# A hybrid decoder layer on one core: the second norm's 1/rms moved from the operand of the expert scores to the scores themselves

## The chip, the core and the metric

The program runs on one core of a Trainium2 chip. The metric is device time in microseconds, from start to end of one execution. Three runs of the kernel before took 4057.06, 4062.6 and 4065.22 us; the median is 4062.6.

The engines named here: TensorE (PE in the rows; PEld its weight loads), VectorE (DVE), ScalarE (ACT), GpSimd (POOL), SyncE (SP). Each works through its own instructions in order. DMAs are issued from the queues of SP, ScalarE (ACTq) and GpSimd.

## The reference

One layer of a decoder for 512 tokens of width 2048, all float32, and a final norm:

```python
h = rms_norm(x, norm_mix)
hq, hf, hi, hog, mq, mkv, mkr, ga, gb = split(h @ w_in)
o_a = hgrn2_branch(hq, hf, hi, hog, ...)            # (512, 1024)
o_b = mla_branch(mq, mkv, mkr, ...)                 # (512, 1024)
y = sigmoid(ga) * (o_a @ w_a) + sigmoid(gb) * (o_b @ w_b)
x = x + y @ w_o
x = x + peer_ffn(rms_norm(x, norm_ffn), peer_wq, k1, k2, u_tab, v_tab)
hp = rms_norm(x, norm_ple)
x = x + sigmoid(hp @ w_pg) * (p @ w_pe)
return rms_norm(x, norm_final)
```

`peer_ffn` on the normalised h: queries q = h @ peer_wq, for 8 heads two halves of 128; scores of the halves against 128 keys each; the best 16 of each half, of their 256 sums the best 16; a softmax over these gives the gates. An expert is a row of two tables of 16384 x 2048: the result is the sum over the chosen experts e of gate_e * gelu(u_e . h) * v_e.

## The kernel before

**Precision and weights.** A float32 matrix product is made of three products of rounded parts (`mm3`, L151 to L153): each operand is split into a rounded high part and the rest, the low part. A block of weights is 128 x 2048; it comes in two halves of 512 KB (L107, on SP's queue, `raw`), ScalarE rounds each half (L115, `hi`) and VectorE subtracts (L116, `lo`). There are four tiles of each kind, so two blocks. A block of 16 chunks with 256 columns is 48 products on TensorE.

**Two halves of the tokens.** After the mixers, the tokens go in two halves of 256, A and B. Half A goes through `merge_half` (gates, `w_a`, `w_b`), `residual_half` (`w_o`, x1 = x + y @ w_o), `embed_half` (`w_pe`), and `scores_half` (`wq`, keys). Of half A the first 160 tokens are served by gathering expert rows (128 in `eA`, 32 more in `eX`), the others (NE = 96) and half B (together ND = 352) by dense products over all experts. The order of this part is chosen by the framework's scheduler. Half B then follows under a written order (`manual_schedule`): gates of half B from `xB` (`w_ga`, `w_gb`, 16 blocks each), merge, residual, embeddings, scores. `ahead.step()` loads two blocks ahead and splits one ahead; `run_late()` issues what the block before left over (evacuations, splits); `background()` issues a share of a list `todo`: the top-16 work of 128 tokens (`prep_A`, then `prep_B`), and dot products of gathered rows with h (`dot_u`, L929). `phase` spreads the costs of the list over a number of blocks: here one list over 80 blocks, with `NEARLY` = 26 row dot products mixed into `prep_B`.

**The norm around which the change lies.** `residual_half` writes x1 to its own tile (L690), adds up squares (L235, L236) and stores x1 (L692). `embed_half` multiplies the embeddings of its half and, amid them, sums the squares over the features on TensorE (L206), makes 1/rms (`rstd_cols`) and spreads it over rows (`rows_of`, L215 to L220). Only then `h_chunk` (L723) makes t = x1 * gain * (1/rms) chunk by chunk, and `split` (L158, L159) its high and low part for the scores. `rows_of_h` (L829 to L834) later adds high and low parts of half A again and transposes them to rows (`hrow`, `hrowX`) for the gathered experts.

**Mixers' outputs.** In the second 16 gate blocks of half B, `mixed` (L646) issues on ScalarE's queue the load of a mixer output of 128 x 256 and splits it at once (L158, L159, into `ohB`, `olB`).

**After that.** 128 blocks of `uT` (dense z for ND tokens), with the rest of the row dot products and the gate matrices; then 16 groups of 8 blocks `vB`, with all 160 row updates (L1222), and the last norms and gate. Short-lived tiles of up to 128 x 512 come from `t2()`, a ring of six.

Of the kernel before, what the change touches and what calls it, by code (L numbers as in the profile page):

```python
# [10 lines left out]
F32 = mybir.dt.float32  # L11
# [9 lines left out]
T = 512  # L21
# [29 lines left out]
def kernel(ctx: ExitStack, tc: tile.TileContext, a, dbg=None):  # L51
# [218 lines left out]
    pe_s = [[dram.tile([128, 2, H], F32, name=f"pe{h}_{i}") for i in range(8)] for h in range(2)]  # L270
# [408 lines left out]
    def residual_half(hf, yh, yl, x1, sq):  # L679
        s = slice(hf * H, hf * H + H)  # L680
        for mt in range(16):
# [15 lines left out]
    def p_half(hf, ph, pl):  # L697
        for k in range(2):
            r = t2()[:, :H]
            nc.sync.dma_start(r, a["pT"][k][:, hf * H:hf * H + H])  # L700
            split(ph[:, k], pl[:, k], r)

    def embed_half(hf, ph, pl, sq, rr):

        for i in range(2):
            w = block(a["w_pe"][i])
            for m in range(0, 8, 2):
                ps = mx()
                for c in range(2):
                    for k in range(2):  # L710
                        mm3(ps[:, c * H:c * H + H], *w.part((m + c) * 2 + k, 16), ph[:, k], pl[:, k], k == 0, k == 1)
                t = t2()
                S.activation(t, ps, AF.Copy)
                nc.scalar.dma_start(flat(pe_s[hf][i * 4 + m // 2]), t)
                if (i, m) == (0, 2):
                    rc = rstd_cols(sums_over_features(sq.acc), D, "rc_ffn")
                if (i, m) == (1, 2):
                    rows_of(rc, rr)
            done()

    def h_chunk(k, x1, rr, hh, hl, kept=None):
        t = t2()[:, :H]
        V.scalar_tensor_tensor(t, x1[:, k], g_ffn[:, k:k + 1], rr, op0=OP.mult, op1=OP.mult)  # L723
        split(hh, hl, t)
        if kept is not None:
            nc.scalar.dma_start(kept, t[:, NA + NX:])

    def scores_half(hf, hh, hl):
# [3 lines left out]
        def keys(i, q):  # L732
# [782 lines left out]
```

## Time and profile before

| | |
|---|---|
| median of 3 runs | 4062.6 us |
| the profiled execution | 4065.97 us, its span 4064.2 us, mean granted clock 0.986 |
| TensorE busy | 3948.1 us (97% of the span), 24921 products |
| VectorE busy | 2946.7 us (73%) |
| ScalarE busy | 1744.0 us (43%) |
| GpSimd busy | 528.8 us (13%) |
| DMA | 1013.75 MB, 249 GB/s over the span |

TensorE's busy time counts products that overlap, so a busy stretch need not be one at full rate; the granted clock (PEclk, 1.00 for 2.4 GHz, 0.50 for 1.2) is a mean over a stretch. The boundaries of the windows below are those of the stages: first half's residual (985.6 to 1076.1), its embeddings and scores (to 1202.9), gates of the second half (to 1441.9; the second 16 blocks from about 1318), merge (to 1548.2), residual (to 1641.0), embeddings and scores (to 1788.1; the scores alone at their steady rate from 1701.9), and the groups of `vB` (2841.1 to 3862.0).

### The profile page before, as it was taken

Reading aid. Unit: us, or ns where it says so; the run is one execution under the profiler, and the core shown is the slowest. Engines: PE = TensorE matmul, PEld = TensorE weight load, DVE = VectorE, ACT = ScalarE, POOL = GpSimd, SP = SyncE. Lnnn points to the kernel's source line nnn. Section 1 sums busy time; section 2 is a strip of 40 time slices with the busy share of each in tenths; the row PEclk is TensorE's granted clock in tenths of the full one; section 3 lists DMA queues with packets and bytes.
Section 4 is the critical chain, followed back from the end, with each engine's and each line's share of the span. In section 5 each row is a group of like instructions: output and inputs, shape, how many; then the busy total and the mean of one; then the engine's idle time right before and its main releaser. Section 6 shows DMA issues by size and latency. Waiting matters only on the chain. (4 is left out here: it accounts for less than half of the span.)

```text
span 4064.2 us, 63784 instructions
## 1 busy us (share of the span) xinstructions
PE 3948.1 (97%) x24921; PEld 3742.2 (92%) x24921; DVE 2946.7 (73%) x4421; ACT 1744.0 (43%) x2800; POOL 528.8 (13%) x326
## 2 busy tenths in 40 slices
PE   9999999999989789899999999999999999999998
PEld 7878788899989789799999999999999999999986
DVE  5352565556638588768989898886898898889844
ACT  5242443445434334445455456663333333333443
POOL 0000000000000011012222222221222232222000
PEclk9999999999999999899999999999999999999999
DMA  5222234367766678688888888889999999999632
GB/s 211 93 78 94 68 113 130 127 202 238 225 191 192 213 264 277 228 288 291 304 320 305 307 300 315 325 309 350 355 360 354 345 358 359 363 344 357 212 117 96
DMA packets 317772, 1013.75 MB, mean 249 GB/s; under 512 B 32544, under 2 KB 134432, under 8 KB 274592
## 3 DMA queue, kind: packets, MB, share of 16 engines
q1 hardware_dynamic: 226624, 596.33, 43.4%
q0 software_dynamic: 46080, 335.56, 21.5%
q10 hardware_dynamic: 44768, 77.79, 5.1%
q8 instruction: 197, 3.23, 0.3%
q14 instruction: 103, 0.84, 0.1%
HBM read 933.27 MB, written 76.28 MB: 248 GB/s over the span
## 5 line engine op out<-in xcount | busy, mean ns | idle before, releaser
L116 DVE TENSOR_TENSOR lo<-raw,hi 128x1024 fp32r<-128x1024 f32 x970 | 1168.6, 1221 | 671.0 <-ACT hi L115 666.1
L115 ACT ACTIVATE hi<-raw 128x1024 fp32r<-128x1024 f32 x970 | 1015.7, 1056 | 1227.4 <-PE acc L152 891.0
L151 PE MATMUL acc<-hBh,hi 128*128 128x352 f32 (+1 forms) x2304 | 746.8, 324 | 3.1 <-ACT hBh L158 2.5
L153 PE MATMUL acc<-hBh,lo 128*128 128x352 f32 (+1 forms) x2304 | 742.1, 322 | 0.5 <-DVE lo L116 0.5
L152 PE MATMUL acc<-hBl,hi 128*128 128x352 f32 (+1 forms) x2304 | 739.2, 321 | 0.2
L922 POOL DMA_INDIRECT row<-in_peer_u_dram,eA x128 | 211.8, 1655 | 2351.8 <-DVE eA L942 1394.2
L151 PEld LDWEIGHTS acc<-hBh,hi 128*128 128x128 f32 x2304 | 436.7, 190 | 7.4 <-ACT hBh L158 7.4
L152 PEld LDWEIGHTS acc<-hBl,hi 128*128 128x128 f32 x2304 | 435.9, 189 | 3.0 <-DVE hBl L159 3.0
L153 PEld LDWEIGHTS acc<-hBh,lo 128*128 128x128 f32 x2304 | 435.1, 189 | 0.8 <-DVE lo L116 0.8
L151 PE MATMUL acc<-ahx,hi 128*128 128x352 f32 x1024 | 335.3, 327 | 4.1 <-DVE x L1231 4.1
L153 PE MATMUL acc<-ahx,lo 128*128 128x352 f32 x1024 | 333.9, 326 | 1.9 <-DVE lo L116 1.9
L151 PE MATMUL acc<-ah,hi 128*128 128x352 f32 x1024 | 334.7, 327 | 0.1
L152 PE MATMUL acc<-al,hi 128*128 128x352 f32 x1024 | 330.9, 323 | 3.4 <-DVE al L159 3.4
L153 PE MATMUL acc<-ah,lo 128*128 128x352 f32 x1024 | 333.5, 326 | 0.7 <-DVE lo L116 0.7
L152 PE MATMUL acc<-alx,hi 128*128 128x352 f32 x1024 | 331.0, 323 | 1.7 <-DVE alx L159 1.7
L151 PE MATMUL acc<-xh,hi 128*128 128x256 f32 (+1 forms) x912 | 305.0, 334 | 0.0
L153 PE MATMUL acc<-xh,lo 128*128 128x256 f32 (+1 forms) x912 | 304.7, 334 | 0.0
L152 PE MATMUL acc<-xl,hi 128*128 128x256 f32 (+1 forms) x912 | 304.0, 333 | 0.0
L1222 DVE SCALAR_TENSOR_TENSOR hrow<-row,zA,hrow 128x2048 f32<-128x2048 f32 x127 | 297.9, 2346 | 1.1
L929 DVE SCALAR_TENSOR_TENSOR row<-row,hrow 128x2048 f32<-128x2048 f32 x128 | 291.6, 2281 | 8.5 <-DMA row<-in_peer_u_dram,eA 8.5
L922 POOL DMA_INDIRECT row<-in_peer_v_dram,eA x128 | 211.2, 1650 | 575.2 <-DVE hrow L1222 510.1
L151 PEld LDWEIGHTS acc<-ahx,hi 128*128 128x128 f32 x1024 | 193.7, 189 | 4.8 <-issue 4.6
(430 smaller groups left out, 8110.9 us busy)
## 6 DMA issues: line engine op xcount, KB each, us to landing
raw<-in_uT_dram SPq DMA_DIRECT2D x256, 512.0 KB, 7.1
raw<-in_vB_dram SPq DMA_DIRECT2D x256, 512.0 KB, 8.8
raw<-in_w_ga_dram SPq DMA_DIRECT2D x64, 512.0 KB, 4.2
raw<-in_w_gb_dram SPq DMA_DIRECT2D x64, 512.0 KB, 4.5
raw<-in_w_o_dram SPq DMA_DIRECT2D x64, 512.0 KB, 5.0
raw<-in_wq_dram SPq DMA_DIRECT2D x64, 512.0 KB, 5.1
z_s<-t ACTq DMA_DIRECT2D x128, 176.0 KB, 6.9
G_s<-stage ACTq DMA_DIRECT2D x11, 2048.0 KB, 14.1
```

The costliest lines, as they stand in the source:

```text
L115: S.activation(hi, raw, AF.Copy)
L116: V.tensor_tensor(lo, raw, hi.bitcast(F32), op=OP.subtract)
L151: TE.matmul(out, lhsT=lh, rhs=rh, start=start, stop=False)
L152: TE.matmul(out, lhsT=lh, rhs=rl, start=False, stop=False)
L153: TE.matmul(out, lhsT=ll, rhs=rh, start=False, stop=stop)
L922: G.indirect_dma_start(out=row, out_offset=None, in_=tab, in_offset=bass.IndirectOffsetOnAxis(ap=e[:, s:s + 1], axis=0))
L929: V.scalar_tensor_tensor(row, row, 1.0, hrowX if x else hrow, op0=OP.mult, op1=OP.mult, accum_out=z[:, s:s + 1])
L1222: V.scalar_tensor_tensor(o, row, c[:, s:s + 1], o, op0=OP.mult, op1=OP.add)
```

## The change

- In `residual_half` the sum stays in its short-lived tile `r`; the operand of the scores is split from it at once, with the gain and without 1/rms (`split` with a gain: L161, L162 of the new file). The x1 tile and `h_chunk` go.
- `scores_half` multiplies the scores by 1/rms when they leave the accumulator (`norm()`). A function `beside(i)` is called at each of its 16 blocks. For half A it prepares one chunk of `xB` (before, after all scores), makes 1/rms in block 0, and transposes rows in blocks 4 to 10 with 1/rms as the scale of the evacuation; the 96 dense tokens go out as four stores on SP's queue, not sixteen on ScalarE's. For half B it adds high and low part, multiplies by the spread 1/rms and splits again, for the dense products.
- Embeddings of both halves are multiplied once, in half B, on 512 columns (before: per half, on 256).
- `mixed` issues the load and returns the split, which is put among the late work two blocks on.
- `prep_A` is spread over 20 blocks, `prep_B` with `NEARLY` = 36 row steps over 60. Dot products and updates become one list (`row_op`): 36 in the blocks of half B, 136 beside `uT` (before 134), among them the first 12 updates, and 148 beside `vB` (before 160).
- Some pools change sides.

```diff
@@ mixed
         r = t2()[:, :H]
         nc.scalar.dma_start(r, (oa_s + ob_s)[i][:, hf * H:hf * H + H])
-        split(oh[:, i], ol[:, i], r)
+        return lambda: split(oh[:, i], ol[:, i], r)
@@ residual_half
-                V.tensor_tensor(x1[:, mt], ps, r, op=OP.add)
-                sq.add(x1[:, mt])
-                nc.scalar.dma_start(x1_s[mt][:, s], x1[:, mt])
+                V.tensor_tensor(r, ps, r, op=OP.add)
+                split(hh[:, mt], hl[:, mt], r, g_ffn[:, mt:mt + 1])
+                sq.add(r)
+                nc.scalar.dma_start(x1_s[mt][:, s], r)
@@ scores_half
-                        S.activation(t, sc[b], AF.Copy)
+                        S.activation(t, sc[b], AF.Copy, scale=norm()[:, b:b + 1])
...
             w = block(a["wq"][i])
+            beside(i)
@@ half A
+    def beside_A(k):
         r = t2()[:, :H]
         nc.sync.dma_start(r, a["xT"][k][:, H:])
         V.scalar_tensor_tensor(r, r, g_mix[:, k:k + 1], rr_mix[:, H:], op0=OP.mult, op1=OP.mult)
         split(xBh[:, k], xBl[:, k], r)
...
+        if k == 0:
+            rcA.append(rstd_cols(sums_over_features(sq.acc), D, "rc_ffnA"))
...
+            rows_of(rcA[0], rrA[0])
+        if k >= 4 and k % 2 == 0 and k < 12:
+            rows_of_h(hrow, 0, NA, k // 2 - 2, rcA[0][:, :1])
+            dense_h(k // 2 - 2)
+        if 4 <= k < 8:
+            rows_of_h(hrowX, NA, NX, k - 4, rcX)
@@ order of half B
-    NEARLY = 26
-    todo = prep_A() + merge(prep_B(1), [(2.5, dot_u)] * NEARLY)
-    NB2 = 80
-    todo = phase(NB2, todo)
+    NEARLY = 36
+    todo = phase(20, prep_A()) + phase(60, merge(prep_B(1), [(2.5, row_op)] * NEARLY))
@@ gates of half B
-            if n:
-                mixed(i, 1, oh, ol)
+            if len(mix) > 1:
+                late.append(mix.pop(0))
+            if n and i or not n and i == 15:
+                mix.append(mixed(n * i, 1, oh, ol))
+    late.extend(mix)
@@ embeddings, now once for both halves
+    for m in range(16):
+        if m % 8 == 0:
+            w = block(a["w_pe"][m // 8])
+        pe_ps = mx()
+        for k in range(2):
+            mm3(pe_ps, *w.part((m % 8) * 2 + k, 16), ph[:, k], pl[:, k], k == 0, k == 1)
+        t = t2()
+        S.activation(t, pe_ps, AF.Copy)
+        nc.scalar.dma_start(pe_s[m], t)
+        if m == 3:
+            rcB = rstd_cols(sums_over_features(sq.acc), D, "rc_ffnB")
+        if m == 10:
+            rows_of(rcB, rrB)
@@ half B
+    def beside_B(k):
+        t = t2()[:, :H]
+        V.tensor_tensor(t, huh[:, k].bitcast(F32), hul[:, k].bitcast(F32), op=OP.add)
+        V.tensor_tensor(t, t, rrB, op=OP.mult)
+        split(hBh[:, k, NE:], hBl[:, k, NE:], t)
```

ScalarE in the second 16 gate blocks of half B, before: the gate of the block (L1080, L1081), the load of a mixer output (L646), its split (L158), then the roundings of the next weights (L115).

```order
L1080 ACTIVATE t_11636<-acc 128x256
L1081 DMA gb_0_139<-t_11636 128x256
L646 DMA t_11688<-oa_156 128x256
L158 ACTIVATE ohB<-t_11688 128x256
L115 ACTIVATE hi_76<-raw_72 128x1024
L115 ACTIVATE hi_77<-raw_73 128x1024
L1080 ACTIVATE t_11698<-acc 128x256
L1081 DMA gb_1_140<-t_11698 128x256
```

The same place now; `t_11402` was loaded from `oa_155` three gates earlier.

```order
L1074 ACTIVATE t_11476<-acc 128x256
L1075 DMA gb_0_139<-t_11476 128x256
L646 DMA t_11536<-oa_156 128x256
L115 ACTIVATE hi_76<-raw_72 128x1024
L115 ACTIVATE hi_77<-raw_73 128x1024
L1074 ACTIVATE t_11544<-acc 128x256
L1075 DMA gb_1_140<-t_11544 128x256
L646 DMA t_11600<-oa_157 128x256
L115 ACTIVATE hi_78<-raw_74 128x1024
L115 ACTIVATE hi_79<-raw_75 128x1024
L1074 ACTIVATE t_11608<-acc 128x256
L1075 DMA gb_2_141<-t_11608 128x256
```

The split of a mixer output no longer follows its load; two blocks of roundings stand between them.

VectorE late in the second residual, before: low halves of weights (L116), the residual sum (L690), the sum of squares (L236), a row dot product (L929).

```order
L116 TENSOR_TENSOR lo_82<-raw_74,hi_78 128x1024
L116 TENSOR_TENSOR lo_83<-raw_75,hi_79 128x1024
L690 TENSOR_TENSOR x_B<-acc,t_14585 128x256
L236 TENSOR_TENSOR sqacc<-sqacc,t_14660 128x256
L929 SCALAR_TENSOR_TENSOR row_7017,zA<-row_7017,hrow 128x2048
```

The same place now.

```order
L116 TENSOR_TENSOR lo_82<-raw_74,hi_78 128x1024
L116 TENSOR_TENSOR lo_83<-raw_75,hi_79 128x1024
L691 TENSOR_TENSOR t_14451<-acc,t_14451 128x256
L162 SCALAR_TENSOR_TENSOR hul<-t_14451,gains,huh 128x256
L236 TENSOR_TENSOR sqacc<-sqacc,t_14528 128x256
L915 SCALAR_TENSOR_TENSOR row_6474,zA<-row_6474,hrow 128x2048
```

One instruction more per block (L162), which needs ScalarE's high part; the sum is written to the short-lived tile.

SP's queue in the first-half scores, before: halves of `wq` and nothing else.

```order
L107 DMA raw_72<-in_wq_dram 128x1024
L107 DMA raw_73<-in_wq_dram 128x1024
L107 DMA raw_74<-in_wq_dram 128x1024
L107 DMA raw_75<-in_wq_dram 128x1024
L107 DMA raw_72<-in_wq_dram 128x1024
```

The same place now: one chunk of the second half's input per block, and four stores of dense tokens, of which one stands here.

```order
L107 DMA raw_72<-in_wq_dram 128x1024
L806 DMA t_9432<-in_xT_dram 128x256
L107 DMA raw_73<-in_wq_dram 128x1024
L800 DMA hd_s<-t_9445 128x384
L806 DMA t_9518<-in_xT_dram 128x256
L107 DMA raw_74<-in_wq_dram 128x1024
L107 DMA raw_75<-in_wq_dram 128x1024
L107 DMA raw_72<-in_wq_dram 128x1024
L806 DMA t_9590<-in_xT_dram 128x256
```

The loads of weights now share SP's queue with instructions that wait for short-lived tiles and for VectorE.

## Rows read from the trace of the kernel before

**Rows 1.** Windows by stage: window, its length, busy us of engines, clock, DMA.

```profile
985.60:1076.10 90.50, 90.50 (x771) 90.50 (x770) 52.11 (x66) 39.41 (x50) 0.00 (x0) 1.00 0.75 231
1076.10:1202.90 126.80, 117.04 (x937) 112.55 (x935) 59.93 (x82) 61.05 (x90) 0.00 (x0) 0.96 0.63 197
1202.90:1441.90 239.00, 202.95 (x1568) 195.75 (x1568) 158.69 (x385) 89.94 (x134) 5.76 (x6) 0.93 0.62 204
1318.00:1441.90 123.90, 99.08 (x729) 93.81 (x727) 70.72 (x124) 40.49 (x62) 5.76 (x6) 0.93 0.63 213
1441.90:1548.20 106.30, 93.55 (x768) 91.91 (x768) 93.58 (x221) 40.46 (x52) 11.76 (x7) 0.98 0.81 271
1548.20:1641.00 92.80, 92.75 (x769) 92.58 (x770) 81.50 (x145) 39.64 (x50) 10.07 (x6) 0.98 0.87 290
1641.00:1788.10 147.10, 131.25 (x936) 123.23 (x934) 97.92 (x132) 64.83 (x100) 15.39 (x10) 0.87 0.69 240
1701.90:1788.10 86.20, 86.20 (x735) 86.20 (x733) 59.47 (x65) 39.73 (x57) 11.84 (x7) 1.00 0.84 295
2841.10:3862.00 1020.90, 1009.01 (x6176) 1004.69 (x6175) 901.68 (x982) 337.98 (x407) 258.88 (x157) 1.00 0.90 340
```

**Rows 2.** ScalarE in order of time, second gate blocks: start, us, operation, [idle before].

```profile
1336.47 0.42 ACT L158 ACTIVATE ohB<-t 128x256 fp32r<-128x256 f32 x1 [4.53 <-DMA t<-oa]
1336.80 1.99 ACT L115 ACTIVATE hi<-raw 128x1024 fp32r<-128x1024 f32 x2
...
1343.95 0.42 ACT L158 ACTIVATE ohB<-t 128x256 fp32r<-128x256 f32 x1 [4.89 <-DMA t<-oa]
...
1415.71 0.42 ACT L158 ACTIVATE ohB<-t 128x256 fp32r<-128x256 f32 x1 [12.01 <-DMA t<-ob]
```

**Rows 3.** TensorE's waits, 1441.9 to 1641: us in total, times, longest.

```profile
PE acc L151 <- DVE t L669: 8.1, 6, 1.8
```

**Rows 4.** TensorE's waits, 1641 to 1788.

```profile
PE mx L206 <- DVE sqacc L236: 7.8, 1, 7.8
PE mx L217 <- DVE t L215: 4.3, 1, 4.3
```

**Rows 5.** VectorE in order of time, chunks before the second scores.

```profile
1672.09 0.48 DVE L723 SCALAR_TENSOR_TENSOR t<-x_B,gains,rrB 128x256 f32<-128x256 f32 x1
1673.05 0.43 DVE L159 TENSOR_TENSOR hBl<-t,hBh 128x256 fp32r<-128x256 f32 x1 [0.48 <-ACT hBh L158]
```

**Rows 6.** Line 833, transposes for rows: ns min/median/max, first and last start.

```profile
L833 PE MATMUL mx<-cst,t x32: 272/273/303, 1224.5 to 1229.0; 128*128 128x128 f32 x32
```

**Rows 7.** VectorE in order of time, first row dot product.

```profile
1403.50 2.29 DVE L929 SCALAR_TENSOR_TENSOR row<-row,hrow 128x2048 f32<-128x2048 f32 x1 [8.51 <-DMA row<-in_peer_u_dram,eA]
...
1406.06 2.40 DVE L116 TENSOR_TENSOR lo<-raw,hi 128x1024 fp32r<-128x1024 f32 x2
```

**Rows 8.** DMA issues: count, KB each, median us to landing.

```profile
t<-in_xT_dram SPq DMA_DIRECT2D x48, 128.0 KB, 5.3
...
scores<-sc ACTq DMA_DIRECT2D x4, 1024.0 KB, 6.9
...
x1s<-x_A ACTq DMA_DIRECT2D x16, 128.0 KB, 4.7
...
x1s<-x_B ACTq DMA_DIRECT2D x16, 128.0 KB, 5.9
```

**Rows 9.** ScalarE in order of time, after the load of the first scores.

```profile
1207.57 0.72 ACT L158 ACTIVATE xBh<-t 128x256 fp32r<-128x256 f32 x2 [4.76 <-DMA sc<-t]
```

**Rows 10.** VectorE in order of time: one top-16 step, from its first row to what follows.

```profile
1232.40 0.47 DVE L846 MAX8 val<-scores 128x8 f32<-128x128 f32 x2
...
1234.75 2.33 DVE L116 TENSOR_TENSOR lo<-raw,hi 128x1024 fp32r<-128x1024 f32 x2
```

**Rows 11.** VectorE in order of time, second residual.

```profile
1635.63 0.43 DVE L236 TENSOR_TENSOR sqacc<-sqacc,t 128x256 f32<-128x256 f32 x1 [0.54 <-ACT t L235]
```

**Rows 12.** VectorE's waits, 2841.1 to 3862.

```profile
DVE zt L1150 <- DMA gt<-G_s: 52.3, 13, 6.0
```

More of the change, by code (lines that the diff above doesn't have):

```diff
@@ L269 @@
     sc_s = [dram.tile([128, 2048], F32, name=f"sc{i}") for i in range(4)]
-    pe_s = [[dram.tile([128, 2, H], F32, name=f"pe{h}_{i}") for i in range(8)] for h in range(2)]
+    pe_s = [dram.tile([128, T], F32, name=f"pe{i}") for i in range(16)]
     hd_s = dram.tile([128, KT, NE], F32, name="hd_s")
@@ L689, in res, with scores_half @@
             def res(mt=mt, ps=ps, r=r):
-                V.tensor_tensor(x1[:, mt], ps, r, op=OP.add)
-                sq.add(x1[:, mt])
-                nc.scalar.dma_start(x1_s[mt][:, s], x1[:, mt])
+                V.tensor_tensor(r, ps, r, op=OP.add)
+                split(hh[:, mt], hl[:, mt], r, g_ffn[:, mt:mt + 1])
+                sq.add(r)
+                nc.scalar.dma_start(x1_s[mt][:, s], r)
             after(res)
             done()
[L697 to L728, printed above, removed]
+    def scores_half(hf, hh, hl, norm, beside=lambda i: None):
         sc = [None, None]
@@ L766, in scores_half @@
         return turn
+    rows_pool = tc.alloc_tile_pool(name="rows_pool", bufs=1, side="left")
+    rows = Ring(rows_pool, 3, [128, D], F32, "row")
+    kpool = tc.alloc_tile_pool(name="kpool", bufs=1, side="left")
+    kk_t = kpool.tile([128, 2, 128], F32, name="kk_t")
+    nc.scalar.dma_start(kk_t, a["kT"].rearrange("h c k -> c h k"))
     opool = tc.alloc_tile_pool(name="opoolA", bufs=1, side="left")
@@ new lines @@
+    rrB = huB.tile([128, H], F32, name="rrB")
+    ppool = tc.alloc_tile_pool(name="ppool", bufs=1, side="right")
+    ph = ppool.tile([128, 2, T], F32R, name="ph")
+    pl = ppool.tile([128, 2, T], F32R, name="pl")
+    for k in range(2):
+        r = t2()
+        nc.sync.dma_start(r, a["pT"][k])
+        split(ph[:, k], pl[:, k], r)
+    sq = SumSq(n=H)
+    residual_half(1, yh, yl, huh, hul, sq)
+    for m in range(16):
+        if m % 8 == 0:
+            w = block(a["w_pe"][m // 8])
+        pe_ps = mx()
+        for k in range(2):
+            mm3(pe_ps, *w.part((m % 8) * 2 + k, 16), ph[:, k], pl[:, k], k == 0, k == 1)
+        t = t2()
+        S.activation(t, pe_ps, AF.Copy)
[4 more added lines that the diff above has]
+            rows_of(rcB, rrB)
+        if m % 8 == 7:
+            done()
@@ L1111 @@
[L1111 to L1115 removed]
+    def beside_B(k):
[3 more added lines that the diff above has]
+        split(hBh[:, k, NE:], hBl[:, k, NE:], t)
+        if k % 4 == 1:
+            t = t2()[:, :4 * NE].rearrange("p (k t) -> p k t", k=4)
+            s = slice(k - 1, k + 3)
+            nc.sync.dma_start(t, hd_s[:, s])
+            late.append(lambda t=t, s=s: split(hBh[:, s, :NE], hBl[:, s, :NE], t))
@@ L1237, in v_products @@
         return ps
-    axpys = NDOT
     NV = (NGRP - 1) * 8
@@ L1326 @@
         pe = t2()
-        for h in range(2):
-            nc.sync.dma_start(pe[:, h * H:h * H + H], pe_s[h][mt // 2][:, mt % 2])
+        nc.sync.dma_start(pe, pe_s[mt])
         cur = ahead.step()
```

176 lines of the change are left out of this document (76 added, 100 removed).

## The prediction

> **What bounds the kernel now.** I read the share of busy time first (the page: TensorE 97% of the span), then the windows by stage, because one average hides where the other 3% lies and where the clock is at its lower level. A stage that nothing holds up is the first pass of the output projection: 90.5 us for 16 blocks of 48 products, clock 1.00, so a block of 256 columns is 90.5 / 16 = 5.66 us and a product 118 ns [rows 1]. Against that yardstick the stages between 1076 and 1788 us are long. The gates of the second half take 239.0 us for 32 blocks, where 32 x 5.66 = 181 would do; the merge takes 106.3 and the second residual 92.8 against 90.5; the stretch of per-layer embeddings and scores of the second half takes 147.1 us, with the clock at 0.87 on average, that is, partly at 1.2 GHz instead of 2.4 [rows 1]. Before 1076 and after 1788 TensorE is nearly always busy. So the chain runs through TensorE, and what can be won are its waits in 712 us (126.8 + 239.0 + 106.3 + 92.8 + 147.1).
>
> Who it waits for differs by stage. In the second half of the gates it is ScalarE: its in-order stream issues the load of a mixer output, then splits that same tile, and stands 4.53 and 4.89 us for the landing before it can round the next weights; the period is 1343.95 - 1336.47 = 7.5 us, where 5.66 would do [rows 2]. In the merge it is VectorE, 93.58 of 106.3 us busy [rows 1], whose late products with the gates keep accumulators occupied: 8.1 us of waits in six places [rows 3]. At the end of the second residual the sum of squares comes late, 7.8 us, and the broadcast of 1/rms 4.3 us [rows 4]; then normalised chunks arrive one by one, a chunk's VectorE, ScalarE, VectorE chain standing 0.48 us inside it each time [rows 5].
>
> **The change, part by part.** The sum is made against the profiled execution (4065.97 us with a span of 4064.2), 3.4 us above the median of the three, 4062.6.
>
> First half, 1076.1 to 1202.9 (126.8 us). The first-half embedding products leave, and no chunk waits for 1/rms any more: the operand of the scores is written inside the residual pass. Left are 16 blocks of 52 products; the second half does 735 in 86.2 us [rows 1], so 6.10 each, 97.6 in all. The 32 transposes for the rows come in; they took 4.5 us at most (1224.5 to 1229.0) [rows 6]. Against it: loads of the second half's input chunk by chunk on SP's queue, five VectorE passes more per few blocks, and groups of transposes that stand in TensorE's order ahead of the VectorE sum they need (two groups in each of two blocks, one in another). TensorE reaches such a group some 1.4 us into its block (12 products), and VectorE's sum follows a rounding that can only end 1.0 + 1.2 us after the block began (halves of 1.99 and 2.40, [rows 2, 7]); I take 1.5 to 2.5 us for each of five waits, 9 us, and 4 for query waits and the start. The input loads take 5.3 us to land [rows 8], inside a block of 6.1, so VectorE waits but TensorE has two blocks in hand. 97.6 + 4.5 + 13 = 115: **-12**. Ends: 106 (no wait) and 127 (all given back).
>
> Gates of the second half (239.0 us). Two costs go. The operand is ready before the stage, and each mixer output is split two blocks after its load is issued; 11.3 us against landings of 4 to 5. Without the stand ScalarE has per block 2.0 for roundings, 0.42 for the split, a sigmoid and two issues, well under 5.66. VectorE has 8 rows here where it had 4, and all of the first block's top-16 in 20 blocks rather than some 26; its 158.69 us [rows 1] grow by 4 x 2.3 and shed the input chunks, which stays under 181. What stays: the load of the first scores still waits for their stores (4.76 us of ScalarE [rows 9]), takes 6.9 us to land [rows 8], and the third block's low halves stand behind two top-16 steps on VectorE. Stores and load make 11 to 13 us after the last score, the steps 4.7 (two of 2.35, [rows 10]), the first two blocks cover 11.3: a wait of 5 to 8 us, with a slow clock behind it 10. The first row dot product still waits for its gather (8.51 us [rows 7]), now with no ScalarE stand beside it: 3 us. 181 + 10 + 3 = 194: **-45**. Ends: 184 and 215.
>
> Merge (106.3 us). VectorE stays the bound; two rows more of 2.3 us (9 for 7), fewer top-16 steps: **+2**; ends -2 and +7. Here the cover is already gone, so any VectorE time counts in full.
>
> Second residual (92.8 us). VectorE has 81.50 us of work [rows 1] and stands 0.54 us per block for ScalarE's square [rows 11], 16 x 0.54 = 9, so it is occupied 90 of 92.8: no slack. In come 15 low halves of 0.48 (the nearest row is the scalar_tensor_tensor of that size [rows 5]), 7.2 us, and two rows, 4.6; out go some top-16 steps. 100: **+7**; ends 93 and 107.
>
> Embeddings and scores of the second half (147.1 us). The products of both halves go together: 96 of 512 columns, at most 96 x 2 x 118 ns = 22.6 us, where half of that stood. The sums are wanted 24 wide products into it and not 24 narrow ones, the four splits of kept rows that stood ahead of them go away, and the scores no longer wait for chunks. 24 + 16 x 6.10 = 122, and 3 for VectorE, whose block (low halves 2.4, two adds and a split 1.3 with a stand of 0.5, background 2.2) comes to 6.4: 125, **-22**. Ends 121 and 140.
>
> Later. 12 rows leave the last big stage (148 for 160) and go into stages that TensorE fills; VectorE there loses 12 x 2.3 = 28 us of 902, where it waits 52.3 us for gate tiles and TensorE idles 12 of 1020.9 [rows 1, 12]: **-4**; ends -12 and 0. The single load of an embedding tile per block at the end I cost at nothing: the products of a block of 512 columns hide it, and without that cover it would be one landing of some 2 us.
>
> Sum: -12 - 45 + 2 + 7 - 22 - 4 = -74. 4065.97 - 74 = 3992 for a profiled execution; 3.4 less, 3989, for the median.
>
> One thing that the diff does not say: the residual's tile `r` is one of six shared temporaries and is now held until its store has landed, not until one VectorE add. The store lands in 4.7 us in the first half and 5.9 in the second [rows 8]. A slot then lives for the load of 5.3, an add of 0.42, an issue and the store of 5.9: about 12 us, 15 with VectorE's queue; three slots in turn make 5.1 us a block, just under 5.66, so I take nothing, with 0 and +94 as ends (below).
>
> The Trainium skill bears on this: "DMA: Bandwidth & Descriptors", section "Anatomy of one DMA", gives a transfer 2.0 us plus its bytes at 436 GB/s, an estimate of 2.3 us for 128 KB, most of it the receipt of the write. By that rule a slot would live some 6 us and the ring would never bind, and the sum would stay as it is; the trace disagrees, with 4.7 and 5.9 us for the stores [rows 8], and the measurement decides, so the rival below keeps its chance and the sum keeps its zero.
>
> **The rivals.**
> 1. Every cover holds: the VectorE waits hide, and the stages take their products' time (106, 184, 104, 93, 121 and -12 later: 116 less at the very best, some 105 with a few waits). For it: ScalarE is under half busy everywhere. Against it: VectorE at 88% in the merge before anything is added. Time 3958.
> 2. VectorE becomes the bound from the gates to the last score, and most of the win turns into its waits: 115 + 205 + 111 + 105 + 136 is 672, 40 less than 712. For it: 10 rows earlier and 16 low halves and adds more, in stages at 88% already. Against: some 165 us of VectorE work in 181 of gates. Time 4022.
> 3. Slower: the ring of six. If lookups and square tiles take so many slots that only two turn over for `r` and for the input chunks, a block there takes 15.2 / 2 = 7.6 us and not 5.66: 1.95 x 48 blocks (two residual passes, first-half scores) = 94 more, 4083. It decides from 74 / 48 = 1.5 us a block. For it: two landings of 5 to 6 us in each slot's life. Against: `r` is reused only every sixth allocation, in the built order three blocks apart.
> 4. The change does not do what it says: behind the 1 MB of scores a mixer load took 12.01 us [rows 2], more than two blocks; if that held throughout, the 39 us of the second gate stretch stay (123.9 for 15.2 blocks of 5.66), 4028. Against: it is once, the others are 4 to 5 us.
>
> **How the numbers follow.** The forecast (3989, own range 3970 to 4008) 0.51; rival 1 0.22; rival 2 0.20; rival 3 0.04; rival 4 0.03. The range reaches to both neighbours: 3955 to 4032. What this kernel's measurement cannot tell from no change is 0.2%, 8 us. Faster 0.95 (forecast and rivals 1, 2 and 4, less 0.01 for the slow tail of rival 2), same 0.02 (that tail and the mild end of rival 3), slower 0.03 (the rest of rival 3).
>
> **What would show it.** Right: in the second gate stretch no ScalarE stand for a mixer load, a period near 5.7 us; between residual and scores of either half no TensorE wait over 3 us; VectorE over 90% in merge and second residual, the latter near 100 us; one TensorE wait of 5 to 8 us in the third gate block. Wrong: SP's loads of weights standing behind a temporary, roundings that wait for weights, or a second residual over 107 us.

## The result and the profile after

The changed kernel takes 3961.6 us (median of 4 runs, 3957.45 to 3965.38) against 4063.9 for the kernel before, measured beside it: 0.9747 of the time, 95% interval 0.9726 to 0.9769. The forecast was 3989, own range 3970 to 4008, stated range 3955 to 4032. The profiled execution took 3957.45 us, span 3955.7, 34.5 less than the 3992 of the sum.

The windows by stage of the kernel after answer to [rows 1]; the columns are the same (length; busy us of TensorE, weight loads, VectorE, ScalarE, GpSimd; clock; DMA).

```profile
983.73:1070.78 87.05, 87.05 (x771) 87.05 (x769) 57.20 (x79) 45.10 (x63) 0.00 (x0) 1.00 0.76 236
1070.78:1178.12 107.34, 105.45 (x868) 101.80 (x867) 63.14 (x91) 55.51 (x86) 0.00 (x0) 1.00 0.63 203
1178.12:1375.06 196.94, 185.65 (x1542) 184.84 (x1541) 157.94 (x389) 85.89 (x114) 13.62 (x10) 0.97 0.75 259
1375.06:1479.38 104.32, 93.61 (x770) 91.99 (x769) 92.67 (x209) 40.11 (x50) 12.69 (x8) 0.98 0.84 290
1479.38:1581.15 101.77, 95.62 (x769) 93.33 (x769) 89.82 (x148) 44.41 (x64) 14.38 (x9) 0.97 0.86 294
1581.15:1617.69 36.54, 28.98 (x104) 22.75 (x103) 18.42 (x29) 16.42 (x26) 3.55 (x3) 0.81 0.87 313
1617.69:1725.80 108.11, 100.00 (x833) 98.63 (x831) 88.53 (x124) 50.69 (x83) 8.43 (x9) 0.98 0.78 260
1725.80:2764.65 1038.85, 1034.24 (x6509) 1029.07 (x6508) 911.83 (x1440) 581.08 (x1198) 229.58 (x136) 1.00 0.87 318
2764.65:3758.55 993.90, 990.37 (x6179) 987.02 (x6177) 875.62 (x969) 339.77 (x406) 212.99 (x145) 1.00 0.90 337
```

Beside the terms of the sum, in us (the lengths before are those of [rows 1], and for the rest differences of the stage boundaries):

| stage | before | forecast | after | off by |
|---|---|---|---|---|
| start to first residual | 985.6 | 985.6 | 983.7 | -1.9 |
| first residual | 90.5 | 90.5 | 87.0 | -3.4 |
| first half's scores (before: and embeddings) | 126.8 | 115 | 107.3 | -7.7 |
| gates | 239.0 | 194 | 196.9 | +2.9 |
| merge | 106.3 | 108 | 104.3 | -3.7 |
| second residual | 92.8 | 100 | 101.8 | +1.8 |
| embeddings and second scores | 147.1 | 125 | 144.7 | +19.7 |
| uT, vB, last gate | 2276.1 | 2272 | 2229.9 | -42.2 |

So the gates, which were the largest term, came as worked out, and two terms failed in opposite directions: the second embeddings and scores won 2 us instead of 22, and the late stages, where 4 were expected, won 46.

TensorE's waits, in windows of the first scores (three rows), the gates, the embeddings (two) and the second scores: us in total, times, longest.

```profile
PE mx L217 <- DVE t L215: 0.8, 1, 0.8
PE mx L707 <- ACT t L731: 0.3, 1, 0.3
PE mx L206 <- DVE sqacc L236: 0.2, 1, 0.2
...
PE acc L153 <- DVE lo L116: 11.2, 3, 6.0
...
PE mx L206 <- DVE sqacc L236: 3.9, 1, 3.9
PE mx L217 <- DVE t L215: 3.7, 1, 3.7
...
PE mx L707 <- ACT t L731: 8.1, 6, 2.7
```

The 13 us that were set against the first half for five waits at the transposes, queries and the start are 5.2 here (107.3 less 97.6 and 4.5), of which 1.3 are waits. No run undoes this part of the change, so its cause is read from these rows alone.

ScalarE in the second gate blocks, answering to [rows 2]: the split of a mixer output stands 0.40 us behind the sigmoid before it, not 4.5 to 4.9 behind a landing.

```profile
1350.60 0.42 ACT L158 ACTIVATE ohB<-t 128x256 fp32r<-128x256 f32 x1 [0.40 <-ACT t L1074]
```

### The profile page after: what moved, and what is told of

The parts are those of the page before. It is cut to its first block, busy times and chain, and to the rows that moved or that the text cites. A ratio compares the mean times of both kernels' runs of the same rounds, so it can differ in the third digit from the quotient of the medians.

```text
span 3955.7 us, 63576 instructions
## 1 busy us (share of the span) xinstructions
PE 3873.2 (98%) x24825; PEld 3677.9 (93%) x24825; DVE 2950.8 (75%) x4439; ACT 1750.3 (44%) x2814; POOL 496.4 (13%) x326
## 5 line engine op out<-in xcount | busy, mean ns | idle before, releaser
L116 DVE TENSOR_TENSOR lo<-raw,hi 128x1024 fp32r<-128x1024 f32 x966 | 1163.7, 1221 | 599.2 <-ACT hi L115 590.7
L115 ACT ACTIVATE hi<-raw 128x1024 fp32r<-128x1024 f32 x966 | 1012.5, 1056 | 1222.1 <-PE acc L152 819.1
L153 PE MATMUL acc<-hBh,lo 128*128 128x352 f32 x2048 | 662.1, 323 | 0.0
L152 PE MATMUL acc<-hBl,hi 128*128 128x352 f32 x2048 | 661.0, 323 | 0.0
L151 PE MATMUL acc<-hBh,hi 128*128 128x352 f32 x2048 | 658.7, 322 | 0.0
L153 PEld LDWEIGHTS acc<-hBh,lo 128*128 128x128 f32 x2048 | 385.5, 188 | 0.0
L151 PEld LDWEIGHTS acc<-hBh,hi 128*128 128x128 f32 x2048 | 385.3, 188 | 0.0
L152 PEld LDWEIGHTS acc<-hBl,hi 128*128 128x128 f32 x2048 | 384.9, 188 | 0.0
L904 POOL DMA_INDIRECT row<-in_peer_v_dram,eA x128 | 188.2, 1470 | 645.3 <-DVE hrow L924 610.5
L153 PEld LDWEIGHTS acc<-ahx,lo 128*128 128x128 f32 x1024 | 192.6, 188 | 3.7 <-DVE lo L116 3.7
```

Of the source, the lines that this page charges most:

```text
L115: S.activation(hi, raw, AF.Copy)
L116: V.tensor_tensor(lo, raw, hi.bitcast(F32), op=OP.subtract)
L151: TE.matmul(out, lhsT=lh, rhs=rh, start=start, stop=False)
L152: TE.matmul(out, lhsT=lh, rhs=rl, start=False, stop=False)
L153: TE.matmul(out, lhsT=ll, rhs=rh, start=False, stop=stop)
L904: G.indirect_dma_start(out=row, out_offset=None, in_=a["peer_v" if v else "peer_u"], in_offset=bass.IndirectOffsetOnAxis(ap=e[:, s:s + 1], ...
```

## The experiments

Stage lengths in us, each from the first product of a stage to the first of the next, in the traces of all that kept the structure of the kernel after:

| kernel | start | first res. | first scores | gates | merge | sec. res. | embed. | scores | uT | vB | end | median |
|---|---|---|---|---|---|---|---|---|---|---|---|---|
| after | 983.7 | 87.0 | 107.3 | 196.9 | 104.3 | 101.8 | 36.5 | 108.1 | 1038.9 | 993.9 | 197.1 | 3961.6 |
| shift_after | 985.4 | 89.6 | 107.1 | 196.2 | 106.2 | 102.1 | 36.2 | 108.0 | 1040.6 | 1000.6 | 201.6 | 3978.1 |
| vrows160 | 984.5 | 90.5 | 107.0 | 196.3 | 107.4 | 101.8 | 35.4 | 108.1 | 1034.2 | 1011.6 | 197.1 | 3975.7 |
| late_sums | 982.9 | 90.5 | 107.1 | 197.0 | 107.6 | 100.8 | 35.2 | 108.2 | 1040.1 | 995.4 | 197.2 | 3964.7 |
| mix_at_once | 984.5 | 90.5 | 106.8 | 235.8 | 108.2 | 102.2 | 35.1 | 108.1 | 1039.3 | 993.5 | 197.1 | 4003.0 |
| nearly26 | 982.7 | 87.0 | 106.5 | 194.1 | 98.9 | 98.3 | 35.9 | 103.7 | 1040.6 | 992.9 | 197.1 | 3946.4 |
| one_list | 983.8 | 90.5 | 107.0 | 194.8 | 111.0 | 104.7 | 34.7 | 114.3 | 1040.3 | 994.2 | 197.1 | 3974.2 |
| ring5 | 983.7 | 90.5 | 107.3 | 199.0 | 124.6 | 103.5 | 37.6 | 109.9 | 1039.6 | 992.6 | 197.1 | 3989.4 |
| quiet | 983.2 | 90.5 | 106.9 | 194.2 | 100.9 | 101.6 | 27.4 | 108.5 | 1041.0 | 989.8 | 197.1 | 3946.3 |
| few_x | 975.8 | 90.5 | 107.1 | 193.8 | 95.7 | 95.1 | 31.3 | 100.3 | 1044.8 | 994.8 | 197.1 | 3936.0 |
| final | 977.2 | 87.0 | 107.8 | 185.8 | 94.3 | 99.0 | 25.3 | 101.3 | 1046.3 | 994.2 | 197.1 | 3923.5 |

The first residual shows what repeats here: 87.0 in three of these kernels and 90.5 in seven, though most of them differ in nothing that runs before it. Its products start 113.3 ns apart in the one case and 117.8 in the other, for the whole stage. In shift_after it is 89.6. The merge differs as much without a cause that is known: 104.3, 107.4 and 107.6 in after, vrows160 and late_sums, none of which changes anything up to it. So 3.4 us of the result may be chance, and a single difference of that size in one stage is not read as an effect below.

### Where the late stages won: the place of the operands, and the rows

**shift_after** and **shift_before** move tiles by 32 unused bytes and change no work.

```
+    off = ctx.enter_context(tc.tile_pool(name="off", bufs=1, side="left"))
+    G.memset(off.tile([128, 8], F32, name="pad_off"), 0.0)
```

In shift_after a second such tile stands in the pool `hr`; in shift_before one in `vwA` and one in `tl`.

> The kernel after with 32 unused bytes put in front of the long-lived tiles on the left of SBUF and at the start of those on the right, nothing else. In the kernel before, most operands of the products after the mixers began 32 bytes past a multiple of 64; in the kernel after the large ones of the two expert phases, the last gate and the first-half residual begin on a multiple of 64; here they begin 32 past again. Theory 1 (the place of the operand sets the rate of the products; it, and not the moved row operations, gave most of the 46 us that the stages after the second scores lost): V groups of 384 products go from 61.4 to 61.9 back to 62.3 us (+20 us in 32), the uT stage +14, the last gate +4.6, first residual +3.4: about 4000 us in all. The latent projections, which no part of the change touches, go from 227 ns back to 234 per 512-column product. Theory 2 (VectorE was relieved by 12 rows and the rate is a matter of load, not of place): no stage moves by more than 2 us, 3962 us.

> The kernel before with 32 unused bytes in three places, so that the operands of the expert phases and the last gate begin on a multiple of 64. Theory 1 (place): uT stage -14, V stage -20, last gate -5: about 4024 us, with V groups at 61.4 to 61.9 us where they took 62.3. Theory 2 (load of VectorE): 4063 us, groups at 62.3.

Measured: shift_after 3978.1 us, 0.9786 of the kernel before (0.9771 to 0.9801), where the kernel after has 0.9747; shift_before 4045.7 against 4065.8, 0.9952 (0.9936 to 0.9968). The same 480 products of the last gate (512 columns), windows of the kernel before, then after, then shift_after:

```profile
3878.01:3990.42 112.41, 112.41 (x483) 90.27 (x482) 51.12 (x60) 41.87 (x52) 0.00 (x0) 1.00 0.37 117
```

```profile
3774.28:3883.51 109.23, 109.23 (x483) 90.27 (x481) 50.93 (x60) 41.88 (x52) 0.00 (x0) 1.00 0.38 120
```

```profile
3787.93:3900.33 112.40, 112.40 (x482) 90.13 (x481) 51.10 (x60) 41.87 (x52) 0.00 (x0) 1.00 0.36 116
```

TensorE is busy throughout, the clock is 1.00 and the weight loads are the same, yet the stretch takes 3.2 us less after, and the 32 bytes give it back. Mean distance between starts of successive products, in ns, from the traces (distances that hold a wait are left out), with the place of the moving operand's first byte, modulo 128, in the built programs:

| products | before | shift_before | after | shift_after |
|---|---|---|---|---|
| latent projections, 512 columns, which no edit touches | 233.3 (96) | 227.0 (0) | 226.9 (0) | 233.3 (32) |
| last gate, 512 | 233.3 (96) | 228.9 (64) | 226.8 (0) | 233.3 (32) |
| uT, 352 | 163.0 (96) | 159.6 (0) | 160.0 (64) | 160.0 (32) |
| vB, 352 | 162.6 (96) | 159.9 (0, 64) | 160.2 (0, 64) | 160.8 (32) |

So the place does set a product's rate: 6.4 ns of 233 for 512 columns, and that with 32 bytes alone. At these rates the place is worth 3 ns x 6144 products = 18 us in uT, 2.4 x 6144 = 15 in vB and 5 in the last gate. These are TensorE's times, an upper bound of what the stages can win by it: uT became 14 us shorter in all, vB 27, and the rest 5. The diff shows it only as pools that change sides and one small tile more on either side (a second `rc_ffn`, `rcX`). Theory 1 is right in kind, but 32 past 64 is not the rule, since uT in shift_after keeps its 160.0: the stage is 1.7 us longer there, not 14, and the time 3978 and not 4000. Nor is the place of the moving operand the whole rule: the first projections, whose moving operand (the rounded weights) begins at 0 and whose weight-load operand (the input) at 96, take 233.3 ns. The first residual's 3.4 us are not of this kind: its moving operand begins at 64 in the kernel before and in the kernel after.

Why shift_before won 20 and not 39: its uT and second scores lose 18.6 us together and its last gate 4.4, but vB stays. Its window in vB and TensorE's waits there (the pads put its lines two to three higher):

```profile
2826.50:3847.60 1021.10, 999.40 (x6178) 992.61 (x6176) 901.16 (x982) 336.14 (x407) 259.19 (x158) 0.99 0.90 341
```

```profile
PE acc L153 <- DVE x L1234: 9.1, 6, 2.5
PE acc L154 <- DVE alx L161: 5.7, 4, 2.4
PE acc L154 <- DVE al L161: 3.6, 5, 1.0
PE acc L155 <- DVE lo L118: 3.4, 7, 0.5
```

Its products are as fast as after, and the 15 us come back, for the most part as waits for VectorE: these rows are 21.8 us in all where the kernel before has 11.7, and with the short stops, all distances over 180 ns hold 36 us more than the steady rate, where before they hold 19. A faster TensorE alone won nothing here, where VectorE carries 901 of 1021 us; in the next run, with as much VectorE work, it won 9.

**vrows160** puts 160 rows beside vB again.

```diff
-    VROWS = 148
+    VROWS = 160
```

> The kernel after with 160 row operations beside vB and 124 beside uT (148 and 136 in the kernel after): the number beside vB is that of the kernel before. Theory 1 (place): V groups stay at 61.4 to 61.9 us and the time at 3962, give or take 6. Theory 2 (the 12 rows taken from VectorE won the 27 us of the V stage): V stage +20 to +27, 3985 us.

Measured: 3975.7 us, vB 17.7 longer and uT 4.7 shorter. Its window and waits in vB:

```profile
2765.24:3776.81 1011.57, 994.60 (x6178) 989.74 (x6177) 901.65 (x982) 336.04 (x407) 259.07 (x157) 1.00 0.90 343
```

```profile
PE acc L152 <- DVE al L159: 5.5, 2, 3.6
PE acc L152 <- DVE alx L159: 5.3, 3, 2.2
PE acc L151 <- DVE x L1237: 3.7, 5, 1.1
PE acc L153 <- DVE lo L116: 2.4, 5, 0.5
```

The waits are 16.9 us, against 3.5 after (2.4 and 1.1). The two theories were put as rivals, and both hold: with faster products and 160 rows vB takes 1021.1 us in shift_before and 1011.6 here, 0 to 9 less than before, and the 12 rows give 17.7 on top. Why these two differ by 9 is open.

### The gates: the mixers' loads

**mix_at_once** undoes that part in the kernel after; **before_mix2** does it alone in the kernel before.

```diff
-            if len(mix) > 1:
-                late.append(mix.pop(0))
-            if n and i or not n and i == 15:
-                mix.append(mixed(n * i, 1, oh, ol))
+            if n:
+                mixed(i, 1, oh, ol)()
```

> The kernel after with each mixer output loaded and split in one go, in the same gate block, as in the kernel before; all else of the change stays. Theory A (ScalarE's stand behind these loads set the period of the second 16 gate blocks): that stretch goes from 98.5 us back to some 115 to 124, the time to 3980 to 3987 us. Theory B (the gates were won by what left VectorE, the input chunks and the early top-16 steps, and the stand would now lie beside other work): stretch under 105 us, time under 3968.

> The kernel before with the split of a mixer output put two blocks behind its load, that part of the change alone. Theory A: the second 16 gate blocks (123.9 us) lose 20 to 30 us and the time is 4034 to 4044. Theory B: VectorE, which still has the input chunks and the old spread of the top-16 steps, takes the place of the stand: at most 10 us, time over 4053.

Measured: mix_at_once 4003.0 us, gates 235.8 (+38.9); before_mix2 4035.5 against 4066.4, ratio 0.9925 (0.9909 to 0.9940), gates 208.7 (239.1 before). Theory A holds both ways, and more strongly than expected. ScalarE in mix_at_once stands again:

```profile
1347.54 0.42 ACT L158 ACTIVATE ohB<-t 128x256 fp32r<-128x256 f32 x1 [4.88 <-DMA t<-oa]
...
1365.04 0.42 ACT L158 ACTIVATE ohB<-t 128x256 fp32r<-128x256 f32 x1 [7.52 <-DMA t<-ob]
```

So of the 42 us of the gates this part gives 30 when done alone and 39 when undone: it is the cause of most of them. The 3 to 12 us that are left must lie with what else changes there, the input chunks and the spread of the top-16 steps; these were not taken apart.

### VectorE from the merge to the scores

**nearly26** and **one_list** change how many rows lie there and how the lists are spread.

```diff
-    NEARLY = 36
+    NEARLY = 26
```

```diff
-    todo = phase(20, prep_A()) + phase(60, merge(prep_B(1), [(2.5, row_op)] * NEARLY))
+    todo = phase(80, prep_A() + merge(prep_B(1), [(2.5, row_op)] * NEARLY))
```

> The kernel after with 26 row operations among the blocks of half B in place of 36, and 146 beside uT in place of 136. Theory A (VectorE's lag sets the second residual, 101.8 us, and both waits in the embeddings, 36.5 us): each row of 2.3 us taken away comes back in the time: residual 95 to 97, embeddings 30 to 33, scores 104 to 106, and the uT stage, where TensorE is 99% busy, takes 10 rows more for at most 5 us: 3945 to 3952 us. Theory B (what is taken from there is paid beside uT in full): 3962, the uT stage 15 to 23 us longer.

> The kernel after with both lists of top-16 and row work spread as one over 80 blocks, as before, with its 36 row operations. Theory A (the dense first 20 blocks cause the wait of 6 us in the third gate block, and the wait of 5 us at the first row operation stays): gates 5 us shorter, and row operations start later and lie closer in merge and residual, which become 4 to 8 us longer: 3960 to 3966 us. Theory B (only the order of the first steps counts): 3957.

Measured: nearly26 3946.4 (0.9708, 0.9695 to 0.9722), better than the kernel after by 15; one_list 3974.2. Ten rows fewer give 2.8 us in the gates, 5.4 in the merge, 3.5 in the residual, 4.4 in the scores and cost 1.7 beside uT: 1.5 us of time for a row that occupies VectorE for 2.3. Each of these is near the spread named above, but they follow the number of rows: with 36 rows (after, vrows160, late_sums) merge, residual and scores take 104.3 to 107.6, 100.8 to 101.8 and 108.1 to 108.2; with 26 (nearly26) 98.9, 98.3 and 103.7; with 14 (few_x, below) 95.7, 95.1 and 100.3. That VectorE's work sets these three stages is shown; the embeddings, expected at 30 to 33, stay at 35.9. With one list the gates win 2 us, less than the spread, and the three later stages lose 12 to 16; by the expectation, because the rows come later and closer. So of the two spreads the one over 20 and 60 blocks is the better, and 36 rows in it are too many.

### The embeddings

**late_sums** and **quiet** are on the two waits of 3.9 and 3.7 us there. What they cost is more than their length: products in order of time on TensorE in the kernel after,

```profile
1590.84 0.99 PE L206 MATMUL mx<-ones,sqacc 128*128 128x1 f32 x4 [3.87 <-DVE sqacc L236]
...
1592.27 0.63 PE L152 MATMUL mx<-pl,hi 128*128 128x512 f32 x1
1592.69 0.63 PE L153 MATMUL mx<-ph,lo 128*128 128x512 f32 x1
```

start 0.43 us apart behind the wait and 0.23 from 1596.5 on. The granted clock is 0.50 in the stretch behind the wait, that is 1.2 GHz, and later 1.00 (0.81 over the whole stage):

```profile
1590.80:1596.50 5.70, 5.67 (x15) 4.67 (x16) 4.63 (x9) 3.34 (x5) 0.94 (x1) 0.50 0.98 355
```

In front of the wait VectorE does this:

```profile
1584.39 2.29 DVE L915 SCALAR_TENSOR_TENSOR row<-row,hrow 128x2048 f32<-128x2048 f32 x1
...
1586.61 2.35 DVE L116 TENSOR_TENSOR lo<-raw,hi 128x1024 fp32r<-128x1024 f32 x2
...
1590.27 0.42 DVE L236 TENSOR_TENSOR sqacc<-sqacc,t 128x256 f32<-128x256 f32 x1
```

```diff
-        if m == 3:
+        if m == 6:
...
-        if m == 10:
+        if m == 14:
```

> The kernel after with the sums of squares of the second half taken at the seventh embedding chunk (fourth before) and 1/rms spread at the fifteenth (eleventh before). Theory A (the second embeddings took 36.5 us and not 24 because TensorE reached both of these before VectorE was there, 3.9 and 3.7 us, and ran the 12 products behind each at 1.2 GHz): both waits gone, 24 us, 3949 us. Theory B (VectorE is the bound of the stretch, and what is not waited for here is waited for in the scores): embeddings 24 us, scores 12 us longer, 3962 us.

Measured: 3964.7, embeddings 35.2. Neither theory: the waits stay in the embeddings, under other names. TensorE's waits there, and VectorE:

```profile
PE mx L151 <- ACT t L1111: 4.5, 3, 3.7
PE mx L217 <- DVE t L215: 4.0, 1, 4.0
```

```profile
1617.82 0.48 DVE L215 TENSOR_SCALAR t<-cst,rc_ffnB 128x128 f32<-128x128 f32 x2 [4.67 <-DMA pe<-t]
```

The first evacuation stands on ScalarE behind the square of the last residual sum, which stands behind VectorE, and TensorE has only four accumulators to run ahead in; the spread of 1/rms then waits for a tile of the ring of six, which an embedding's store holds. Moving the consumer does not help where the producer is late.

**quiet** (26 rows) takes away what stands in front of the producer.

```diff
+        seen[0] += 1
+        if 63 <= seen[0] <= 66:
+            return
         at[0] += 1
```

> The kernel with 26 row operations among the blocks of half B, in which the last two residual blocks and the two embedding blocks issue no background work either (it is spread over 56 other blocks). Theory A (the row operation of 2.3 us and the top-16 steps that stand on VectorE ahead of the last sum of squares and of the spread 1/rms make TensorE's two waits in the embeddings, 3.9 and 4.3 us with 26 rows): both fall under 2 us and the embeddings go from 35.9 to 27 to 31 us, the time from 3946 to 3938 to 3943. Theory B (the waits are the lag of the residual's own chain, low halves, sum, square, and background work is beside the point): embeddings 34 to 36, time 3944 to 3948.

Measured: 3946.3, embeddings 27.4, TensorE's waits there:

```profile
PE mx L206 <- DVE sqacc L236: 1.0, 1, 1.0
PE mx L217 <- DVE t L215: 0.8, 1, 0.8
```

Theory A has the cause: both waits are 1 us or less, and 8.5 us are gone with them. Its time fails: merge, residual and scores take 10.1 us more, since the same work lies there now. That is theory B of late_sums one level up: the sum of VectorE's work from merge to scores decides.

### The ring of six

**ring5**, for the rival that was slower.

```diff
-    def t2(name="t2", bufs=6):
+    def t2(name="t2", bufs=5):
```

> The kernel after with five short-lived tiles in the ring in place of six. Theory A (the ring was near its limit: a slot of the residual now lives for a load, an add and a store, some 12 to 15 us, and three slots in turn made 5.1 us a block): with one fewer the residual and the first scores exceed their 5.66 us, 0.5 to 1 us a block, and the time rises by 20 to 45 us, to 3982 or more. Theory B (the slots turn over with much to spare and the ring never came into it): each stage within 2 us, 3962.

Measured: 3989.4 us, +28: the size of theory A, and not its place. The residuals are 90.5 and 103.5, the first scores 107.3; the merge goes from 104.3 to 124.6. In the merge of ring5, TensorE's largest wait and SP's:

```profile
PE acc L151 <- DVE t L669: 26.1, 8, 6.2
...
SPq L657 <- DVE t L673: 66.3, 7, 12.5
```

In the merge of the kernel after SP waits too, but TensorE far less:

```profile
PE acc L151 <- DVE t L669: 4.8, 4, 1.5
...
SPq L657 <- DVE t L673: 39.2, 12, 7.0
```

SP's loads of gate tiles wait for slots in both. With five tiles the weights that stand behind them in SP's queue come late too. The queue, and the largest such waits of ScalarE and VectorE, in the merge of ring5:

```profile
1404.12 13.08 SPq L657 DMA_DIRECT2D t<-ga  x2
1417.30 0.86 SPq L107 DMA_DIRECT2D raw<-in_w_a_dram  x2
...
ACT hi L115 <- DMA raw<-in_w_a_dram: 28.8, 13, 6.3
...
DVE lo L116 <- ACT hi L115: 21.2, 11, 4.6
```

In the merge of the kernel after these two waits are 1.8 and 1.4 us. So ScalarE waits for weights, VectorE for ScalarE, and TensorE for VectorE's late products with the gates. With five tiles these are the signs that the prediction named for being wrong, a load of weights behind a temporary and roundings that wait for weights, and they stand in the merge, not in the residuals and scores that rival 3 counted. So a ring that is too short does cost time here; a ring of seven or more does not fit beside the tiles of the mixers and was not run.

### Together

**few_x** (14 rows, and 32 bytes in front of the input tiles on the right) and **final** (that, the quiet blocks, and the first top-16 steps from the third block on).

```diff
-    todo = phase(20, prep_A()) + phase(60, merge(prep_B(1), [(2.5, row_op)] * NEARLY))
+    first_steps = prep_A()
+    todo = first_steps[:1] + [(2, lambda: None)] + phase(18, first_steps[1:]) + phase(56, merge(prep_B(1), [(2.5, row_op)] * NEARLY))
```

> The kernel after with 14 row operations among the blocks of half B (158 beside uT) and, apart from that, with 32 unused bytes in front of the input tiles on the right of SBUF, so that these begin on a multiple of 64. Rows: if each row operation in the merge, second residual and scores costs its VectorE time, merge 94 to 97, residual 94 to 96, scores 101 to 104 (98.9, 98.3 and 103.7 with 26), and beside uT, where VectorE then has 970 us of work in 1040, 3 to 15 us more: 3930 to 3945. Otherwise these stages stay as with 26, and uT pays. Place: some 1900 products of 512 columns in the first 890 us take 233 ns; if their rate goes by where the operands begin, 227 ns and 12 us less before 890; if not, the same 889 us. Together 3920 to 3933 if both hold.

> All that helped, together: 14 row operations among the blocks of half B, the input tiles on a multiple of 64, no background work in the last two residual blocks and the embeddings, and, new, the first top-16 steps from the third gate block on (18 blocks for the list, not 20), so that they no longer stand on VectorE ahead of the third block's low halves while the scores are still being loaded. Theory A (that wait of 6.0 us, 8.0 with the slow products behind it, is the order of VectorE's queue alone): gates from 193.8 to 185 to 188 us; embeddings from 31.3 to 25 to 28, of which 1 to 3 come back in the residual and the scores; 3936 to 3922 to 3930. Theory B (the steps packed closer push VectorE over a block's 5.65 us, or the work left out of the embeddings comes back in full): gates 191 or more, time 3932 to 3938.

Measured: few_x 3936.0, with the rows as expected and 6.8 us less before the first merge, where 12 were expected: the 512-column products with rounded weights as moving operand go from 233.3 to 230.2 ns, with nothing moved but the input, their weight-load operand; those with the input as moving operand stay (233.3 and 233.4) although it begins on a multiple of 64. More than half of the 6.8 us lies where the expectation had not looked: the 1536 products of 256 columns with the input as moving operand go from 118.3 to 115.0 ns and take 186.9 us where they took 190.6. final 3923.5, ratio 0.9642 (0.9624 to 0.9660), 1% below the kernel after. Its gates take 185.8 and its embeddings 25.3: theory A, though of the 6.0 us that the embeddings win against few_x 4.9 come back in the residual and the scores, more than the 1 to 3 expected. In the kernel after, the first top-16 step stood on VectorE, in front of the third block's low halves, until the scores had landed:

```profile
1190.66 0.49 DVE L830 MAX8 val<-scores 128x8 f32<-128x128 f32 x2 [10.09 <-DMA scores<-sc]
```

and in the gates of final one wait of TensorE is left:

```profile
PE acc L153 <- DVE lo L116: 2.3, 1, 2.3
```

## Why the prediction was right, and where not

- **The time.** 3961.6 lies in the stated range, but below the forecast's own (3970 to 4008) and next to rival 1. That is luck in part: the late stages won 42 us more than the sum gave them, in good part by a cause that the prediction did not have, the place of the tiles,, and 20 us of the second embeddings and scores went the other way. Without the late 42 the time would have been about 4004.
- **The signs** that were to show it: no ScalarE stand for a mixer load, blocks of 5.65 us in the second gate stretch (all but two) and a wait of 6.0 us in the third gate block came. No wait over 3 us between residual and scores did not hold in the second half (3.9 and 3.7 us), nor did VectorE over 90% in merge and second residual (89% and 88%).
- **The yardstick** of 5.66 us a block held where nothing hinders: 28 of the 32 gate blocks take 5.65 us, two 6.2 and 6.4, and two, with the waits, 13.7 and 12.4. It was one of two rates: the same residual ran at 5.44 after.
- **First half** (115, measured 107.3, low end 106): the five waits at the transposes did not occur. I put 1.5 to 2.5 us on each from the place in TensorE's order; TensorE's waits there are 1.3 us in all. The edge "no wait" was the case, with no run that takes this part alone.
- **Gates** (194, measured 196.9): the mixers' loads are shown by undoing and by doing alone. The two waits that were to stay are 6.0 and 5.0 us, with their slow products 8.0 and 6.7; I had 10 and 3.
- **Merge** (+2, measured -2): at its lower end, and no more than the spread of this stage.
- **Second residual** (100, measured 101.8): the size came, the place only in part. VectorE is busy 89.82 of 101.77 us and stands 8.1 more for ScalarE's high part, so it is occupied for 98 of them, though the busy share alone stays under the 90% I named. But of the 11.3 us above 16 x 5.65 some 7.4 lie in the first two blocks, where TensorE waits for the last sum of the merge and then runs slowly; seven blocks then take 5.65 or 5.75 although they hold the added low half, and the last seven take 6.0 to 6.5. So "no slack" was too strong: the lag that the merge leaves costs more here than the added work. nearly26 and few_x confirm that VectorE's work sets it: with 14 rows every block but the first two takes 5.65. TensorE's waits in this stage after:

```profile
PE acc L151 <- ACT yhB L158: 4.2, 1, 4.2
PE acc L153 <- DVE lo L116: 1.7, 5, 0.5
```

- **Embeddings and second scores** (125, measured 144.7, outside the end of 140): the step that failed. I wrote that the sums "are wanted 24 wide products into it" and took the products' 22.6 us as the stage. VectorE comes out of the residual late, by a row of 2.3 us and low halves of 2.35, so both waits remain, 3.9 and 3.7 us, and the products behind them run at half the clock: 36.5 us where I had 24. In the scores, 108.1 where I had 101, the query's evacuation is late six times (8.1 us): ScalarE stands 4.2 us for the sum of a chunk, in front of the roundings and of that evacuation. With 26 and 14 rows these waits fall to 3.9 and 2.8 us, so the lag behind them is VectorE's again; that it reaches TensorE by way of ScalarE is read from the rows below. I had the chunk's stand on VectorE (0.5 us), not on the engine that waits for it.

```profile
1652.73 0.42 ACT L158 ACTIVATE hBh<-t 128x256 fp32r<-128x256 f32 x1 [4.21 <-DVE t L1128]
1653.05 1.99 ACT L115 ACTIVATE hi<-raw 128x1024 fp32r<-128x1024 f32 x2
...
1657.11 0.38 ACT L731 ACTIVATE t<-acc 128x256 f32<-128x256 f32 x1 [0.40 <-ACT t L713]
```

- **Later** (-4, end -12, measured -46): the other step that failed. TensorE's idle time of 12 us in vB bounded what 12 rows could win, and the rate of the products was taken as given. Both were too narrow: the rows are worth 17.7 us in vB (and cost 4.7 beside uT), and the place of the tiles changes the rate. The pool sides stood in the diff, and I passed over them.
- **The rivals.** Rival 1 has the time (3958), and not its reason: not every cover held, the late stages made up for it. Rival 2's mechanism is real from the merge to the scores. Rival 3's ring exists, with five tiles and in the merge. Rival 4 did not happen; its 39 us are 37.9 by its own terms (123.9 less 15.2 x 5.66). The stores of x1 land in 5.1 us after (4.7 and 5.9 in [rows 8]). By the Trainium skill, "DMA: Bandwidth & Descriptors", section "Anatomy of one DMA — SWDGE (gpsimd) path", the estimate was 2.3 us; the fit of that section was measured on DMAs that GpSimd issues, and these stores go out from ScalarE's queue. The traces differ from one transfer of 128 KB to another: 4.7 to 5.9 us for these stores, 2.3 for a load of the embeddings in the kernel before. They decide, and nothing hung on the estimate.

## What to carry to other kernels

A load whose result the same in-order engine splits at once cost that engine the whole landing here: ScalarE stood 86 us in 15 blocks of the kernel before. Issue it two steps ahead, and check what else stands in that queue. Where VectorE was busy for 88% of a stage, a row of 2.3 us cost 1.5 us of time: added work is not free there. Expect that a wait removed in one place comes back in the next stage with the same engine. Before a gain or a loss is put down to an edit, compare the distance between products in stages that the edit does not touch: if tiles have moved, it may be that.

## What the runs showed of the hardware

- Products at the full clock have more than one distance: 226.8 to 227.0 or 233.3 ns for 512 columns, decided by 32 bytes of place; 113.3 or 117.8 for 256, in the same stage of kernels that are alike up to it. The Trainium skill, "TensorE: Matmul & The Clock Gate", section "Back-to-back issue gap", gives one value for each for a product by itself, 518 and 262 cycles, at 2.4 GHz 216 and 109 ns: in these streams, each product with a weight load, the trace has 11 to 18 and 4 to 9 ns more, and the measurement decides.
- What of the place decides is open. For the moving operand of the last gate, the latents and the expert phases 0 modulo 128 was always fast and 96 always slow, 32 slow for 512 columns and hardly for 352, 64 fast in uT and between the two in the last gate (228.9). For the input tiles 64 as moving operand was slow at 512 columns (233.4) and faster than 96 at 256 (115.0 for 118.3). The place of the weight-load operand counts too: with the moving operand at 0, 233.3 ns with the other at 96 and 230.2 at 64. What else decides the rate at 256 columns is open: the first residual has 113.3 and 117.8 at the same place.
